# The low parts of the streamed weights beside a recurrence: made by VectorE and not by GpSimd

## The chip, the cores and the metric

The kernel runs on one core of one Trainium2 chip. The metric is the device time of one execution in microseconds, from all inputs in HBM to the whole output in HBM. The engines are named as in the profile: PE is TensorE (PEld its weight loads), DVE is VectorE, ACT is ScalarE, POOL is GpSimd, SP is SyncE, which issues the DMAs. Each engine takes its own queue of instructions in order and waits on semaphores for the others.

## The reference

Two layers on 512 tokens of width 2048, all in float32. The first projects the normed input to 8336 columns (`ab_w_in`) and feeds two branches, 16 heads of attention with a forget gate and 16 heads of a recurrence; both are gated and go through `ab_w_out`. The second is a gated MLP with spatial mixing (`c_w_in`, `c_w_out`). Each layer ends with a norm, a residual and a gated projection. What matters here is the recurrence, for each head a 64x64 state `S` that every token changes:

```python
def step(S, inp):
    r_t, w_t, k_t, v_t, kk_t, a_t = inp
    sa = jnp.einsum('bhij,bhj->bhi', S, kk_t)
    S = S * w_t[:, :, None, :] - sa[..., None] * (kk_t * a_t)[:, :, None, :] + v_t[..., None] * k_t[:, :, None, :]
    y = jnp.einsum('bhij,bhj->bhi', S, r_t)
    return S, y
```

and the projection `proj = xn @ ab_w_in[j]`, whose columns are independent of each other, so that some can be computed while the recurrence runs.

## The kernel before

**Dense products.** Every float32 product with a weight is made of three products of a rounded type: weight and input are split into a high part and a low part, and PE adds high x high, high x low and low x high (L165, L166, L167 in `dense_fm`). The inputs `xh` and `xl` are split once and stay. The weights are streamed: `stream` loads 128x1024 float32 values per DMA (`raw`, two buffers), ACT rounds 128x512 of them to the high part (`whi`, L154), and the engine `self.weng` subtracts it from `raw` to give the low part (`wlo`, L155). `whi` and `wlo` have four buffers each. One such piece serves four k-steps, that is twelve matmuls of `dense_fm`. A column block of 128 takes four pieces.

**Which engine makes the low part.** `self.weng` is an attribute that is set in a few places. In `enter` it is GpSimd for the first two column blocks, but for their first piece; at the end of `enter` (L1243) it becomes VectorE, and so it is for the column blocks that `rwkv_all` makes ahead of its loop (`start(0)`, `start(1)`, one `ahead()`). Right ahead of the loop over the recurrence, L682 sets it to GpSimd. L1269, after `rwkv_all`, sets it back to VectorE for all the rest.

**The recurrence.** The tokens of a pair of heads are taken in eight chunks of 64. For each chunk `rwkv_chain` has three products in a row, each of which needs the one before through a copy out of PSUM: L536 (tile `ch` from the state `SV`), copied to `Bs` by DVE (L539, partitions 0 to 63) and ACT (L540, partitions 64 to 127); L543 with `Bs`, copied to `UV` in the same way (L545 and L546); L551 with `UV`, from which DVE makes the next state `SV` in two halves (L555, two instructions), which the L536 of the next chunk needs. L560 and L561 make the chunk's outputs. Beside the chain the next pair is prepared: `rwkv_prep` (among others L360, L361, L364 and on GpSimd L366, a 128x512 product `a`), `rwkv_ops` (L397, L398, L400, L403, which write `BK` and `AR`; L397 needs the `a` of L366), `rwkv_head` (L423 on PE from `BK` and `AR`), `rwkv_inverse` (the small 32x32 matmuls L490, with the copies L499, L507, L508, L516 and on GpSimd the masks L483) and `rwkv_tokens` (on GpSimd L449, L467 and L468).

**What sets the order.** PE never runs the chain alone. `rwkv_all` gives each step a place on a scale of beats, one beat for each k-step of `dense_fm`, and `beat()` runs the steps that are due, so chain steps and dense matmuls alternate on PE; two chain steps are three beats apart. The dense work is that of the pairs to come (`start(pr + 2)`) and of columns whose results are wanted later (`ahead()`, which parks them in HBM). The program is then scheduled by a list scheduler: it keeps a clock of its own costs and puts on each engine's queue what is ready and has the highest priority. High and low parts have the priority `WPRI` (150000), the chain's copies 60 and the copies of the inverse 80, so that a low part that is ready goes ahead of the chain. After this the queues are fixed.

Of the kernel before, what the change touches and what calls it, by code (L numbers as in the profile page):

```python
# [70 lines left out]
class Net:  # L71
# [522 lines left out]
    def rwkv_all(self, dense, k0, wp, ps):  # L594

        nc, tc = self.nc, self.tc
        sts = {}

        def start(pr):
            sts[pr] = st = {}  # L600
            st["r"] = self.t(wp, [P, T], "r")
            st["k"] = self.t(wp, [P, T], "k")
            st["v"] = self.t(wp, [P, T], "v")
            for c0, m, dst in ((C_RK, 8, st["k"]), (C_R, 0, st["r"]), (C_RV, 16, st["v"])):
                acc = k0 if (pr, m) == (0, 8) else dense(c0 + pr * P)
                with tc.high_priority(HP):
                    self.shifted(acc, m + pr, dst, wp)

        def ahead():

            c0 = AHEAD[len(self.ahead)]
            acc = dense(c0)
            y = self.t(self.wsp, [P, T], "wlo")
            nc.scalar.copy(y, acc)
            self.ahead[c0] = self.gd[len(self.ahead)]
            nc.sync.dma_start(self.ahead[c0], y)

        prep = lambda pr: self.rwkv_prep(pr, sts[pr], wp, ps)
        ops = lambda pr, h: self.rwkv_ops(sts[pr], h, wp)
        head = lambda pr, h: self.rwkv_head(sts[pr], h, wp, ps)  # L620
        tokens = lambda pr, h: self.rwkv_tokens(sts[pr], h, wp, ps)
        inverse = lambda pr: self.rwkv_inverse(sts[pr], wp, ps)
        chain = lambda pr, h: self.rwkv_chain(sts[pr], h, wp, ps)
        fin = lambda pr: self.rwkv_fin(pr, sts[pr], wp, ps)

        start(0)
        with tc.high_priority(HP):
            for gen in (prep(0), ops(0, 0), ops(0, 1)):
                list(gen)
            for h in range(NG):  # L630
                list(head(0, h))
            list(inverse(0))
            list(tokens(0, 0))
        start(1)
        for _ in range(EARLY[0]):
            ahead()

        todo = []

        def put(pr, n, step):  # L640
            todo.append((1 + 2 * WIN * pr + n, step))

        def run(pr, make, *args_places):
            *args, places = args_places
            gen = []

            def step():
                if not gen:
                    gen.append(make(*args))
                next(gen[0], None)  # L650

            for n in places:
                put(pr, n, step)
            put(pr, places[-1], lambda: [0 for _ in gen[0]])

        def begin(pr):
            S0 = sts[pr]["hf", 0]["SV"][:, 0]
            for q in range(2):
                nc.gpsimd.memset(S0[q * 64 : q * 64 + 64, q, :], 0.0)
            sts[pr]["Yt"] = self.t(wp, [P, T], "Yt")  # L660

        for pr in range(8):
            put(pr, CHAIN[0][0], lambda pr=pr: begin(pr))
            run(pr, tokens, pr, 1, TOKENS[1])
            for h in range(NG):
                run(pr, chain, pr, h, CHAIN[h])
            if pr > 0:
                run(pr, fin, pr - 1, FIN)
            if pr < 7:
                if pr == 0:  # L670
                    run(pr, prep, 1, PREP1)
                    run(pr, ops, 1, 0, OPS1[0])
                run(pr, ops, pr + 1, 1, OPS[1] if pr else OPS1[1])
                for h in range(NG):
                    run(pr, head, pr + 1, h, (HEAD if pr else HEAD1)[h])
                run(pr, inverse, pr + 1, STAGE)
                run(pr, tokens, pr + 1, 0, TOKENS[0])
            if pr < 6:
                run(pr, prep, pr + 2, PREP)
                run(pr, ops, pr + 2, 0, OPS[0])  # L680
        self.weave(sorted(todo, key=lambda x: x[0]))
        self.weng = nc.gpsimd  # L682
        for pr, n in enumerate(BESIDE):
            if pr < 6:
                start(pr + 2)
            for _ in range(n):
                ahead()
        self.weave([])
        with tc.high_priority(HP):
            list(fin(7))  # L690
        for _ in range(EARLY[1]):
            ahead()
# [630 lines left out]
```

## Time and profile before

| what | us |
|---|---|
| median of three runs (2384.97 to 2393.15) | 2385.49 |
| the profiled execution | 2386.83 |
| its span, first to last instruction | 2385.1 |
| PE, PEld busy | 2325.8, 1904.0 |
| DVE, ACT, POOL busy | 1172.5, 1046.1, 504.3 |
| mean granted clock of PE | 0.993 |

A row of the order of time gives start, duration, engine, line, operation and tiles; in brackets stands how long the engine stood idle before it and which instruction ended that. A row of waits reads: engine, tile and line of the waiting instruction, those of the one it waited for, then the sum in us, how often, and the longest. A group of instructions gives its count, the busy sum and the mean in ns, and then the engine's idle time ahead of it. A row of stretches gives start and end, length, busy time of PE, PEld, DVE, ACT and POOL with counts, the granted clock of PE, the share of the DMA engines and GB/s. The recurrence lies between 120 and 780 us of the span.

### The profile page before, as it was taken

The page shows a single profiled execution, that of the slowest core. Times are in us where ns is not written, and L with a number is a line of the kernel's source. Part 1 is how long each engine was busy: PE and PEld are TensorE (multiplying, and loading weights), DVE is VectorE, ACT ScalarE, POOL GpSimd, SP SyncE. Part 2 cuts the span into 40 slices and gives each one's busy share as a digit, 9 for nine tenths or more (in the row PEclk, how much of TensorE's full clock was granted, in tenths as well). Part 3 has the DMA queues.
Part 4 walks back from the last instruction along what each step waited for, and adds up shares of the span by engine and source line. Part 5 has one row for each costly group of instructions (what it writes and reads, how often), then busy time and mean ns, then how long its engine had stood idle before and what let it go on. Part 6 is the DMA issues. An engine that isn't in the chain of part 4 may idle for free.

```text
span 2385.1 us, 39010 instructions
## 1 busy us (share of the span) xinstructions
PE 2325.8 (98%) x15356; PEld 1904.0 (80%) x15356; DVE 1172.5 (49%) x2336; ACT 1046.1 (44%) x2135; POOL 504.3 (21%) x488
## 2 busy tenths in 40 slices
PE   6999999999999999999999999999999999999999
PEld 5777877877888777787887888888888888887888
DVE  8644455544511577765227453326544443226433
ACT  5434545554543466665335443323333332335322
POOL 4123443444444000000013110002442000112000
PEclk9999999999999999999999999999999999999999
DMA  6222222223234533326333323233443333232332
GB/s 206 69 77 62 74 79 67 75 59 85 68 89 117 147 93 89 90 83 211 99 102 102 97 89 106 89 97 105 111 111 98 97 97 98 94 104 83 118 114 90
DMA packets 300310, 235.03 MB, mean 99 GB/s; under 512 B 11453, under 2 KB 251214, under 8 KB 299102
## 3 DMA queue, kind: packets, MB, share of 16 engines
q1 hardware_dynamic: 300126, 232.54, 33.3%
q8 instruction: 121, 1.98, 0.3%
q14 instruction: 63, 0.52, 0.1%
HBM read 216.47 MB, written 16.02 MB: 97 GB/s over the span
## 4 chain that ended last, share of the span: by engine, by line
PE 87%; DVE 5%; ACT 3%; issue 1%; DMA 1%; POOL 1%; DVEq 0%; SPq 0%; ACTq 0%; POOLq 0%
PE mm L165 15%; PE mm L167 15%; PE mm L166 15%; PE mm L912 6%; PE mm L914 6%; PE mm L913 6%; PE mm L198 5%; PE mm L200 5%; PE mm L199 5%; PE tm L490 2%; PE tm L828 1%; ACT whi L154 1%; PE mm L1147 1%; PE ch L536 1%; PE tm L423 1%
## 5 line engine op out<-in xcount | busy, mean ns | idle before, releaser
L154 ACT CAST whi<-raw 128x512 fp32r<-128x512 f32 x724 | 447.6, 620 | 883.9 <-PE mm L166 383.3
L155 DVE TENSOR_TENSOR wlo<-raw,whi 128x512 fp32r<-128x512 f32 x566 | 410.2, 727 | 701.3 <-ACT whi L154 686.7
L165 PE MATMUL mm<-xh,whi 128*128 128x512 f32 x1136 | 475.6, 419 | 1.8 <-DVE k L321 1.8
L167 PE MATMUL mm<-xh,wlo 128*128 128x512 f32 x1136 | 452.0, 398 | 0.0
L166 PE MATMUL mm<-xl,whi 128*128 128x512 f32 x1136 | 447.6, 394 | 0.8 <-issue 0.8
L155 POOL TENSOR_TENSOR wlo<-raw,whi 128x512 fp32r<-128x512 f32 x158 | 214.0, 1359 | 260.9 <-ACT whi L154 119.5
L167 PEld LDWEIGHTS mm<-xh,wlo 128*128 128x128 f32 x1136 | 214.7, 189 | 47.8 <-issue 0.2
L165 PEld LDWEIGHTS mm<-xh,whi 128*128 128x128 f32 x1136 | 215.7, 190 | 38.1 <-DVE k L321 1.9
L166 PEld LDWEIGHTS mm<-xl,whi 128*128 128x128 f32 x1136 | 216.0, 190 | 34.1
L165 PE MATMUL mm<-yh,whi 128*128 128x512 f32 x576 | 225.9, 392 | 0.0
L167 PE MATMUL mm<-yh,wlo 128*128 128x512 f32 x576 | 224.3, 389 | 0.0
L166 PE MATMUL mm<-yl,whi 128*128 128x512 f32 x576 | 224.2, 389 | 0.0
L1069 POOL TENSOR_TENSOR accq<-accq,sq 128x512 f32<-128x512 f32 x42 | 56.5, 1346 | 607.1 <-ACT sq L1067 541.8
L914 PE MATMUL mm<-xh,wlo 128*128 128x512 f32 x384 | 149.5, 389 | 0.0
L912 PE MATMUL mm<-xh,whi 128*128 128x512 f32 x384 | 149.4, 389 | 0.0
L913 PE MATMUL mm<-xl,whi 128*128 128x512 f32 x384 | 149.4, 389 | 0.0
L167 PEld LDWEIGHTS mm<-yh,wlo 128*128 128x128 f32 x576 | 108.1, 188 | 22.9
L166 PEld LDWEIGHTS mm<-yl,whi 128*128 128x128 f32 x576 | 108.2, 188 | 22.0
L165 PEld LDWEIGHTS mm<-yh,whi 128*128 128x128 f32 x576 | 108.1, 188 | 22.0
L198 PE MATMUL mm<-whi,xh 128*128 128x512 f32 (+1 forms) x320 | 111.2, 347 | 0.0
L200 PE MATMUL mm<-whi,xl 128*128 128x512 f32 (+1 forms) x320 | 110.9, 347 | 0.0
L199 PE MATMUL mm<-wlo,xh 128*128 128x512 f32 (+1 forms) x320 | 110.9, 347 | 0.0
(362 smaller groups left out, 3868.4 us busy)
## 6 DMA issues: line engine op xcount, KB each, us to landing
raw<-in_ab_w_in_dram SPq DMA_DIRECT2D x130, 512.0 KB, 3.9
raw<-in_c_w_in_dram SPq DMA_DIRECT2D x96, 512.0 KB, 3.8
raw<-in_ple_w_gate_dram SPq DMA_DIRECT2D x64, 512.0 KB, 3.9
raw<-in_ab_w_out_dram SPq DMA_DIRECT2D x32, 512.0 KB, 3.9
raw<-in_c_w_out_dram SPq DMA_DIRECT2D x32, 512.0 KB, 3.9
gd<-wlo SPq DMA_DIRECT2D x21, 256.0 KB, 2.3
vT<-gd SPq DMA_DIRECT2D x21, 256.0 KB, 3.4
xt<-in_x_dram SPq DMA_DIRECT2D x4, 1024.0 KB, 8.4
```

Of the source, the lines that this page charges most:

```text
L154: nc.scalar.copy(hi[:, : m * n], src)
L155: self.weng.tensor_tensor(lo[:, : m * n], src, f(hi[:, : m * n]), ALU.subtract)
L165: nc.tensor.matmul(acc, hi, xhi[k], start=(k == 0), stop=False)
L166: nc.tensor.matmul(acc, hi, xlo[k], start=False, stop=False)
L167: nc.tensor.matmul(acc, lo, xhi[k], start=False, stop=(k == nk - 1))
L198: nc.tensor.matmul(accs[m][:, :n], xh, hi, start=(k == 0), stop=False)
L199: nc.tensor.matmul(accs[m][:, :n], xh, lo, start=False, stop=False)
L200: nc.tensor.matmul(accs[m][:, :n], xl, hi, start=False, stop=(k == nk - 1))
L912: nc.tensor.matmul(accs[j], hi[:, js], xhi[k], start=(k == 0), stop=False)
L913: nc.tensor.matmul(accs[j], hi[:, js], xlo[k], start=False, stop=False)
L914: nc.tensor.matmul(accs[j], lo[:, js], xhi[k], start=False, stop=(k == nk - 1))
L1069: eng.tensor_tensor(accq, accq, sq, ALU.add)
```

## The change

One line goes, so that VectorE stays the engine of the low parts through the recurrence:

```diff
         self.weave(sorted(todo, key=lambda x: x[0]))
-        self.weng = nc.gpsimd
         for pr, n in enumerate(BESIDE):
             if pr < 6:
                 start(pr + 2)
```

Inside the loop and in what follows it in `rwkv_all` 38 column blocks are made, each of four pieces: 152 low parts change their engine. The scheduler orders the queues anew with its costs for the other engine. GpSimd's queue keeps its other instructions in their order (but for one L590), DVE's queue has 152 more, and those of PE and ACT differ at some places. What the order is at two of them:

**Place A**, at the end of a pair's first half, when the next pair is prepared; the same order comes back in three pairs (near 222, 380 and 534 us of the trace). DVE's queue before, where `SV_1586` is the state, `T_2451` the operand of the small matmuls:

```order
L360 TENSOR_SCALAR gn_2395<-a_2254,col_136_517,omka_616 128x512
L400 SCALAR_TENSOR_TENSOR AR_144_536<-kk_2317,Pd_2485 64x4x64
L361 TENSOR_TENSOR k_1551<-k_1551,gn_2395 128x512
L397 TENSOR_TENSOR BK_484_2522<-a_2254,sg_2467 64x4x64
L364 SCALAR_TENSOR_TENSOR rkb_2412<-r_1550,col_136_517,k_1551 128x512
L507 STREAM_TRANSPOSE T_2451<-tm_467_2418 128x256
L398 TENSOR_TENSOR BK_484_2522<-k_1551,sg_2467 64x4x64
L555 SCALAR_TENSOR_TENSOR SV_1586<-SV_1586,PC_831,ch_2458 64x64 x2
L397 TENSOR_TENSOR BK_484_2522<-a_2254,sg_2467 64x4x64
```

and of the changed kernel:

```order
L361 TENSOR_TENSOR k_1551<-k_1551,gn_2395 128x512
L397 TENSOR_TENSOR BK_484_2522<-a_2254,sg_2467 64x4x64
L364 SCALAR_TENSOR_TENSOR rkb_2412<-r_1550,col_136_517,k_1551 128x512
L507 STREAM_TRANSPOSE T_2451<-tm_467_2418 128x256
L398 TENSOR_TENSOR BK_484_2522<-k_1551,sg_2467 64x4x64
L555 SCALAR_TENSOR_TENSOR SV_1586<-SV_1586,PC_831,ch_2458 64x64
L155 TENSOR_TENSOR wlo_2476<-raw_2473,whi_2475 128x512
L155 TENSOR_TENSOR wlo_2529<-raw_2473,whi_2528 128x512
L155 TENSOR_TENSOR wlo_2576<-raw_2573,whi_2575 128x512
L555 SCALAR_TENSOR_TENSOR SV_1586<-SV_1586,PC_831,ch_2458 64x64
L397 TENSOR_TENSOR BK_484_2522<-a_2254,sg_2467 64x4x64
```

Three low parts stand between the two halves of the state. On PE, before:

```order
L551 MATMUL ch_2458<-UV_1585,BKt_1583 128x128
L560 MATMUL ch_2462<-AR_145_537,SV_1586 128x128
L561 MATMUL ch_2462<-GR_879,UV_1585 128x128
L165 MATMUL mm_2472<-xh_85_301,whi_2475 128x512
L166 MATMUL mm_2472<-xl_86_302,whi_2475 128x512
L536 MATMUL ch_2493<-SV_1586,AR_145_537 128x128
L167 MATMUL mm_2472<-xh_85_301,wlo_2476 128x512
```

and changed:

```order
L561 MATMUL ch_2462<-GR_879,UV_1585 128x128
L165 MATMUL mm_2472<-xh_85_301,whi_2475 128x512
L166 MATMUL mm_2472<-xl_86_302,whi_2475 128x512
L490 MATMUL tm_482_2498<-T_2451,A_357_1734 32x32 x15
L167 MATMUL mm_2472<-xh_85_301,wlo_2476 128x512
L165 MATMUL mm_2472<-xh_85_301,whi_2475 128x512
L166 MATMUL mm_2472<-xl_88_307,whi_2475 128x512
L167 MATMUL mm_2472<-xh_85_301,wlo_2476 128x512
L165 MATMUL mm_2472<-xh_85_301,whi_2475 128x512
L166 MATMUL mm_2472<-xl_90_318,whi_2475 128x512
L167 MATMUL mm_2472<-xh_85_301,wlo_2476 128x512
L536 MATMUL ch_2493<-SV_1586,AR_145_537 128x128
```

L536, which needs both halves of the state, has moved behind small matmuls and seven dense ones, the first of which reads `wlo_2476`.

**Place B**, once, early in the recurrence (near 159 us): DVE's queue of the changed kernel from L360 on, where `BK_350` and `AR_146` are what L423 reads. Before, neither low part nor L321 stood ahead of the first L400, which came right behind L360.

```order
L360 TENSOR_SCALAR gn_1659<-a_1607,col_136_517,omka_616 128x512
L155 TENSOR_TENSOR wlo_1844<-raw_1841,whi_1843 128x512
L539 COPY Bs_1713<-ch_1711 64x64
L361 TENSOR_TENSOR k_1263<-k_1263,gn_1659 128x512
L397 TENSOR_TENSOR BK_350_1696<-a_1607,sg_1674 64x4x64
L364 SCALAR_TENSOR_TENSOR rkb_1662<-r_1262,col_136_517,k_1263 128x512
L398 TENSOR_TENSOR BK_350_1696<-k_1263,sg_1674 64x4x64
L545 COPY UV_1251<-ch_1729 64x64
L155 TENSOR_TENSOR wlo_1877<-raw_1841,whi_1876 128x512
L321 SCALAR_TENSOR_TENSOR k_1551<-mm_1553,col_42_136,k_1551 128x511
L400 SCALAR_TENSOR_TENSOR AR_146_538<-kk_1629,Pd_1688 64x4x64
```

On PE the L423 that reads them has moved from behind L543 (chunk's second product) to behind L551:

```order
L551 MATMUL ch_1780<-UV_1251,BKt_1249 128x128
L423 MATMUL tm_361_1738<-AR_146_538,BK_350_1696 128x128 x4
L560 MATMUL ch_1784<-AR_144_536,SV_1252 128x128
L561 MATMUL ch_1784<-GR_855,UV_1251 128x128
L165 MATMUL mm_1759<-xh_85_301,whi_1762 128x512
L423 MATMUL g_1739<-AR_146_538,BK_350_1696 128x128 x4
```

## The prediction

> **What bounds the kernel now.** I read the page first, then the busy time by stretch, then what TensorE (PE) waited for, and last the order of time at its longest waits.
>
> ```profile
> PE 2325.8 (98%) x15356; PEld 1904.0 (80%) x15356; DVE 1172.5 (49%) x2336; ACT 1046.1 (44%) x2135; POOL 504.3 (21%) x488
> ```
>
> PE is busy for 2325.8 of 2385.1 us, so a change on two other engines can only move the 59 us in which PE stands, or the clock at which it runs. The change touches the recurrence, which lies between 120 and 780 us:
>
> ```profile
> 120.00:780.00 660.00, 642.20 (x6994) 518.85 (x6993) 299.36 (x723) 317.67 (x770) 278.21 (x253) 0.98 0.29 79
> ...
> 160.00:170.00 10.00, 7.10 (x31) 5.37 (x30) 9.28 (x18) 2.23 (x6) 5.65 (x4) 0.84 0.29 82
> 170.00:180.00 10.00, 10.00 (x46) 8.03 (x46) 7.79 (x23) 2.33 (x7) 1.29 (x1) 0.82 0.02 6
> 220.00:230.00 10.00, 6.94 (x107) 5.23 (x95) 8.66 (x15) 3.60 (x10) 7.37 (x5) 0.74 0.31 84
> 230.00:240.00 10.00, 10.00 (x81) 8.11 (x78) 2.76 (x8) 4.00 (x10) 0.39 (x1) 0.75 0.18 50
> 530.00:540.00 10.00, 6.86 (x93) 5.08 (x91) 8.64 (x16) 4.27 (x13) 7.38 (x5) 0.94 0.23 62
> 540.00:550.00 10.00, 10.00 (x107) 7.84 (x108) 4.99 (x12) 4.82 (x14) 1.74 (x2) 0.89 0.28 73
> ```
>
> The columns are the length and then the busy time of PE, weight loads, DVE, ACT and POOL, then the granted clock. PE stands 660 - 642.2 = 17.8 us in this stretch. Clock is lost as well, three times right behind a gap: 10 x (0.16 + 0.18) = 3.4 us, 10 x (0.26 + 0.25) = 5.1 us, 10 x (0.06 + 0.11) = 1.7 us, together 10.2 us. So 28 us (1.2%) is all that the change can win. What the 17.8 us waited for, in that stretch:
>
> ```profile
> PE ch L536 <- DVE SV L555: 10.8, 6, 3.1
> PE tm L423 <- DVE BK L398: 2.2, 1, 2.2
> PE ch L543 <- ACT Bs L540: 1.9, 5, 0.7
> PE pp L280 <- ACT a L338: 1.3, 1, 1.3
> PE ch L551 <- ACT UV L546: 1.2, 3, 0.4
> ```
>
> No wait is for a low part: POOL makes them in time. PE waits for the chain's own copies on DVE. The largest looks like this (start, duration, engine; place A):
>
> ```profile
> 219.45 1.93 POOL L366 TENSOR_TENSOR a<-kk,a 128x512 f32<-128x512 f32 x1 [11.17 <-DVE gn L360]
> ...
> 221.25 0.38 PE L551 MATMUL ch<-UV,BKt 128*128 128x128 f32 x2
> ...
> 221.35 4.75 POOL L155 TENSOR_TENSOR wlo<-raw,whi 128x512 fp32r<-128x512 f32 x3
> 221.42 1.49 DVE L397 TENSOR_TENSOR BK<-a,sg 64x256 f32<-64x256 f32 x1 [1.18 <-POOL a L366]
> ...
> 222.15 0.40 PE L166 MATMUL mm<-xl,whi 128*128 128x512 f32 x1
> 222.83 0.73 DVE L364 SCALAR_TENSOR_TENSOR rkb<-r,col,k 128x512 f32<-128x512 f32 x1
> 223.49 0.43 DVE L507 STREAM_TRANSPOSE T<-tm 128x256 f32<-128x256 f32 x1
> 223.86 1.11 DVE L398 TENSOR_TENSOR BK<-k,sg 64x256 f32<-64x256 f32 x1
> ...
> 224.90 0.57 DVE L555 SCALAR_TENSOR_TENSOR SV<-SV,PC,ch 64x64 f32<-64x64 f32 x2
> ...
> 225.61 0.77 PE L536 MATMUL ch<-SV,AR 128*128 128x128 f32 x2 [3.06 <-DVE SV L555]
> ```
>
> It comes back at 383 and 537 us:
>
> ```profile
> 383.61 0.46 PE L536 MATMUL ch<-SV,AR 128*128 128x128 f32 x2 [3.13 <-DVE SV L555]
> ...
> 537.67 0.46 PE L536 MATMUL ch<-SV,AR 128*128 128x128 f32 x2 [3.14 <-DVE SV L555]
> ```
>
> That is 9.33 us in three waits; the other three behind L555 share 1.5 us. At A two DVE instructions are stretched while POOL runs three low parts in a row, L397 to 1.49 us and L398 to 1.11. Over the stretch:
>
> ```profile
> L155 POOL TENSOR_TENSOR wlo<-raw,whi 128x512 fp32r<-128x512 f32 x152 | 203.8, 1345 | 242.4 <-ACT whi L154 100.9 <-PE mm L167 82.9 <-PE mm L166 16.8
> ...
> L397 DVE TENSOR_TENSOR BK<-a,sg 64x256 f32<-64x256 f32 x28 | 21.3, 760 | 7.3 <-POOL a L366 7.1
> ...
> L155 DVE TENSOR_TENSOR wlo<-raw,whi 128x512 fp32r<-128x512 f32 x6 | 4.2, 692 | 11.4 <-ACT whi L154 11.4
> ```
>
> **The change, part by part.** It takes 152 instructions (203.8 us) off POOL and puts 152 x 0.692 = 105 us on DVE, whose load in the stretch goes from 299 to some 404 of 660 us (61%), less what the stretching gives back. Neither sum is on the path; what counts is who is late at PE.
>
> *Place A, three times.* In the order of the changed kernel DVE has L397, L364, L507, L398, one half of L555, three low parts, the other half of L555; PE's L536 stands seven dense matmuls and 15 small ones later, and the dense L167 ahead of it needs the first of these low parts. L397 still waits for L366 on POOL, so it starts at 221.42. Unstretched I take 0.42 for L397 and L398 (L507, of as many elements, takes 0.43): 221.84; L364 +0.73 = 222.57; L507 223.00; L398 223.42; half of L555 (0.28) 223.70; first low part 224.39. PE is through L166 at 222.15 + 0.25 = 222.40, stands 0.65 until L507, works 0.35 on the small ones, and stands about 1.0 for the low part. Two more low parts and the second half of L555 end at 224.39 + 1.38 + 0.28 = 226.05, and PE reaches L536 at 224.43 + 7 x 0.23 = 226.04. So 1.7 us stand there and not 3.1: a gain of 1.4 each, 4.2 in all. The bounds: stretched as now, L397 and L398 cost 1.07 + 0.69 more and nothing is won; with every low part behind L555, 3.1 each.
>
> *Place B, once.*
>
> ```profile
> 159.20 0.55 DVE L360 TENSOR_SCALAR gn<-a,col,omka 128x512 f32<-128x512 f32 x1
> ...
> 159.66 1.50 DVE L400 SCALAR_TENSOR_TENSOR AR<-kk,Pd 64x256 f32<-64x256 f32 x1
> ...
> 161.94 1.51 DVE L364 SCALAR_TENSOR_TENSOR rkb<-r,col,k 128x512 f32<-128x512 f32 x1
> ...
> 162.31 0.43 PE L543 MATMUL ch<-Bs,Tfin 128*128 128x64 f32 x2 [0.69 <-ACT Bs L540]
> ...
> 165.24 1.16 PE L423 MATMUL tm<-AR,BK 64*128 64x128 f32 x8 [2.21 <-DVE BK L398]
> ```
>
> PE stands 0.69 + 2.21 = 2.9 us here. Now two low parts (1.4 us) and L321 come ahead of L400, the stretching (1.50 and not 0.4, 1.51 and not 0.73) goes, and the first L423 stands behind L551, nine dense matmuls after L543. From the end of L360 at 159.75 DVE has two low parts (1.38), L539 and L545 (0.21 each), L361, L364 and L321 (0.7 each, as L364 at A), L397, L398 and L400 (0.42 each): 5.2 us, and some 0.4 waiting for L366 on POOL (1.93 from 159.8), so L400 ends near 165.4. PE asks for it at 162.31 - 0.69 + 0.33 + 9 x 0.23 = 164.0 and stands 1.4. The second group of L423 needs L397, L555, L398 and L400 more (1.8 us, 167.2) and is asked for 1.2 us after the first, near 166.6: 0.6 more. That is 2.0 us where 2.9 were, 0.9 won. Bounds: 0 and 2.9.
>
> *The small waits.* The three that share 1.5 us lose the low parts that stretch DVE, and none is put ahead of them there: 1.5 won. Against that, in the order a low part stands right behind a chain copy, and PE wants it soon, at three places a period apart (some 0.2 each) and at three near the end (0.7, 0.7 and 0.1, by the same counting of rows): 2.1 lost.
>
> *Everywhere else.* Of the chain's 240 DVE instructions 100 get one or more low parts between them and the one before. Behind a low part that waits for its high part the whole DVE queue waits, so each can be 0.7 to 1.4 us late. What covers it is the distance on PE:
>
> ```profile
> 300.13 0.40 PE L166 MATMUL mm<-xl,whi 128*128 128x512 f32 x1
> ...
> 300.36 0.40 PE L167 MATMUL mm<-xh,wlo 128*128 128x512 f32 x1
> ...
> 300.60 0.33 PE L543 MATMUL ch<-Bs,Tfin 128*128 128x64 f32 x2
> ...
> 301.25 0.21 DVE L545 COPY UV<-ch 64x64 f32<-64x64 f32 x1
> ...
> 301.49 0.21 ACT L546 COPY UV<-ch 64x64 f32<-64x64 f32 x1 [0.37 <-DVE UV L545]
> ...
> 303.79 0.38 PE L551 MATMUL ch<-UV,BKt 128*128 128x128 f32 x2
> ```
>
> A dense matmul takes 0.23 us; nine or more (2.1 us) lie between a chain product and the one that uses its copy. Here the copy is there at 301.70 and wanted at 303.79: 2.1 us of cover, more than one low part. I take 0; the bounds are 0 and 100 x 0.69 = 69.
>
> *Clock.* All three losses follow gaps of 2.2 to 3.1 us; 383 us has as long a gap and no loss. With gaps of 1.0 to 1.7 they should come less often; no row shows how much, so I take half of 10.2, 5 us, between 0 and 10.2.
>
> [...]
>
> Sum: -4.2 - 0.9 - 1.5 + 2.1 = -4.5 standing, -5 clock, -9.5 in all: the profiled span of 2385.1 becomes 2375.6. That execution took 2386.83, with 1.7 outside the span; the median of the three runs is 1.3 lower, 2385.49, which gives **2376 us**.
>
> [...]
>
> **The rivals.** *The clock comes back whole.* If no gap is long enough any more, -10.2 replaces -5: 2371 us. For it: the losses stand only behind gaps over 2 us. Against it: place B keeps two gaps close together.
>
> *Nothing is won at A and B.* L366 on POOL (1.93 us) and the pile behind it stay; if a low part's high part is late, L536 waits its 3 us: only the small waits move, by +0.6, to 2386 us. For it: L397 waits for POOL in any case. Against it: these three low parts have had their high parts for long (POOL ran them back to back).
>
> *The chain queues behind low parts (slower).* Engines take their queues in order, and elsewhere DVE stands for its high part a lot:
>
> ```profile
> DVE wlo L155 <- ACT whi L154: 686.7, 375, 8.6
> ```
>
> That is 1.8 us a time over the run. It decides from the point where wait plus 0.69 passes the 2.1 us of cover: if a third of the 100 are 0.7 late at PE, 23 us are lost, 2376 + 23 = 2399 us, more if the clock drops too. For it: this row, and that ACT makes its half of every chain copy from the same kind of queue. Against it: the row tells mostly of a DVE that has nothing else to do; ACT's own high parts stand ahead of the chain's copies already, and PE's waits for L540 and L546 are 1.9 + 1.2 us in the whole stretch.
>
> **How the numbers follow.** Forecast (a small win) 0.50, clock whole 0.20, nothing won 0.18, queueing 0.12. Beyond 0.5%, 12 us, a measurement tells from no change: below 2373.6 or above 2397.4. Faster has the clock's 0.20 and a quarter of the forecast's half, 0.32; slower 0.12; same 0.56. The range goes from 2365 (clock whole and 6 us more of the standing) to 2392 (nothing won, and ten of the 100 places 0.7 late).
>
> **What would show it.** Right: at A, PE waits for L507 and then for a low part, 1.7 us together; L397 and L398 near 0.42; DVE near 400 us between 120 and 780, POOL near 74; PE's standing there near 13.5 us. Wrong: waits of PE for L539, L545 or L555 at many places, DVE held for high parts ahead of them, or L536 still 3 us late.

## The result, and the profile after

| | before | changed |
|---|---|---|
| median of six runs each on one chip, us | 2386.50 (2384.97 to 2393.15) | 2373.36 (2369.15 to 2378.73) |
| ratio, 95% interval | | 0.9932 (0.9916 to 0.9947) |
| the profiled execution, us | 2386.83 | 2378.73 |
| its span, us | 2385.1 | 2377.0 |

The changed kernel is 0.68% faster, 13.1 us; 2376 was forecast. On another chip it came to 0.9936 (0.9917 to 0.9955), with a median of 2373.39. The profiled execution is the slowest of the six, and its clock says why (below).

The busy times of the page:

```profile
PE 2326.1 (98%) x15356; PEld 1904.7 (80%) x15356; DVE 1236.8 (52%) x2488; ACT 1046.4 (44%) x2135; POOL 301.3 (13%) x336
```

The recurrence's stretch, and the 120 us ahead of it, which the change doesn't touch (length, then busy time of PE, weight loads, DVE, ACT and POOL, then the granted clock):

```profile
120.00:780.00 660.00, 651.65 (x7071) 524.78 (x7070) 370.04 (x887) 326.75 (x792) 77.26 (x104) 1.00 0.30 83
0.00:120.00 120.00, 96.18 (x927) 70.69 (x928) 85.67 (x191) 53.65 (x101) 34.01 (x46) 0.90 0.42 132
```

PE stands 8.35 us in the recurrence where it stood 17.8, and its clock is whole there. The low parts now cost DVE 0.70 us each, and the stretched instruction of place A is short again:

```profile
L155 DVE TENSOR_TENSOR wlo<-raw,whi 128x512 fp32r<-128x512 f32 x162 | 110.8, 701 | 76.6 <-ACT whi L154 53.5 <-DMA gd<-wlo 9.3 <-PE mm L167 7.8
L397 DVE TENSOR_TENSOR BK<-a,sg 64x256 f32<-64x256 f32 x28 | 11.9, 424 | 7.3 <-POOL a L366 7.1
```

L397 went from 760 to 424 ns. DVE gained 71 us and not 105: its instructions other than low parts add up to 283 us in this stretch and not to 312 (L397 9.4 us less, L398 4.5, L582 4.2). What PE waits for there:

```profile
PE ch L543 <- ACT Bs L540: 2.5, 4, 0.8
PE mm L167 <- DVE wlo L155: 2.4, 4, 1.1
PE tm L490 <- DVE T L507: 1.3, 3, 0.4
PE pp L280 <- ACT a L338: 1.0, 1, 1.0
PE tm L423 <- DVE AR L400: 0.9, 1, 0.9
```

No wait behind L555 is left. Place A in order of time (here at 222.8 us):

```profile
222.83 1.93 POOL L366 TENSOR_TENSOR a<-kk,a 128x512 f32<-128x512 f32 x1 [11.32 <-DVE gn L360]
...
224.80 0.42 DVE L397 TENSOR_TENSOR BK<-a,sg 64x256 f32<-64x256 f32 x1 [1.18 <-POOL a L366]
...
225.14 0.74 DVE L364 SCALAR_TENSOR_TENSOR rkb<-r,col,k 128x512 f32<-128x512 f32 x1
...
225.53 0.40 PE L166 MATMUL mm<-xl,whi 128*128 128x512 f32 x1
225.81 0.43 DVE L507 STREAM_TRANSPOSE T<-tm 128x256 f32<-128x256 f32 x1
226.17 0.38 DVE L398 TENSOR_TENSOR BK<-k,sg 64x256 f32<-64x256 f32 x1
...
226.30 0.69 PE L490 MATMUL tm<-T,A 32*32 32x32 f32 x30 [0.37 <-DVE T L507]
226.48 0.26 DVE L555 SCALAR_TENSOR_TENSOR SV<-SV,PC,ch 64x64 f32<-64x64 f32 x1
...
226.66 1.88 DVE L155 TENSOR_TENSOR wlo<-raw,whi 128x512 fp32r<-128x512 f32 x3
...
227.40 0.50 PE L167 MATMUL mm<-xh,wlo 128*128 128x512 f32 x1 [0.41 <-DVE wlo L155]
...
229.12 0.38 PE L536 MATMUL ch<-SV,AR 128*128 128x128 f32 x2
```

The place has the shape that the order gave: PE waits for L507, then for the first low part, and L536 waits for nothing. But the two waits are 0.37 + 0.41 us, not 1.7.

**Where the time came from.** All waits of PE in the recurrence, added by place from the order of time of both kernels:

| us that PE stands, 120 to 780 us | before | changed | difference | forecast |
|---|---|---|---|---|
| place A, three times | 9.33 | 2.49 | -6.8 | -4.2 |
| place B | 2.90 | 0.86 | -2.0 | -0.9 |
| L536 behind L555, three others | 1.46 | 0 | -1.5 | -1.5 |
| L551 behind ACT's L546 (three of 0.41) | 1.22 | 0 | -1.2 | 0 |
| L543 behind ACT's L540, elsewhere than B | 1.16 | 2.50 | +1.3 | 0 |
| a low part, elsewhere than A | 0 | 1.12 | +1.1 | +2.1 |
| the rest | 1.72 | 1.29 | -0.4 | 0 |
| sum | 17.8 | 8.3 | -9.5 | -4.5 |

The trace also dates each stretch in which PE was granted half its clock (0.50). In one of them, at 232 us of the kernel before, dense matmuls start 0.43 us apart and not 0.23, so such a stretch costs up to half its length. In the recurrence there were 6.8 + 10.2 + 3.4 us of them before and none now. The profiled execution of the changed kernel lost 8.5 us ahead of the recurrence instead, at 81 us (10.2 us long) and 112 us (6.8 us long), where the queues of both kernels are the same. The second profile of the changed kernel lost nothing at either place, so the change doesn't bring it about; experiment 6 takes it up. This is why its own span fell by 8.1 us only.

For the medians the clock has to be taken over all runs. With span times granted clock as the time without the loss, 49 runs of the kernel before on three occasions have a mean of 2368.5 us and 18.8 lost to the clock; the 12 of the changed kernel 2361.0 and 11.3. So the gain is about 7.5 us of work and waits and 7.5 us of clock, 15 us between these means. (Over its whole span PE stands 8.4 and 9.1 us less in the two profiles of the changed kernel, not 9.5: 0.9 to 1.7 us come back ahead of the recurrence, mostly at 105 to 110 us in waits for which the profile shows no releaser, and 0.6 to 1.3 go behind it. What is left between this and 7.5 stays open.)

### The profile page after: what moved, and what is told of

Its sections match the earlier page's. It is cut to its first block, busy times and chain, and to the rows that moved or that the text cites. A ratio compares the mean times of both kernels' runs of the same rounds, so it can differ in the third digit from the quotient of the medians.

```text
span 2377.0 us, 38890 instructions
## 1 busy us (share of the span) xinstructions
PE 2326.1 (98%) x15356; PEld 1904.7 (80%) x15356; DVE 1236.8 (52%) x2488; ACT 1046.4 (44%) x2135; POOL 301.3 (13%) x336
## 4 chain that ended last, share of the span: by engine, by line
PE 87%; DVE 5%; issue 3%; ACT 2%; DMA 0%; POOL 0%; DVEq 0%; SPq 0%; ACTq 0%; POOLq 0%
PE mm L165 15%; PE mm L167 15%; PE mm L166 15%; PE mm L911 6%; PE mm L913 6%; PE mm L912 6%; PE mm L198 5%; PE mm L200 5%; PE mm L199 5%; PE tm L490 2%; PE tm L827 1%; DVE wlo L155 1%; DVE yh L758 1%; PE mm L1146 1%; PE tm L423 1%
## 5 line engine op out<-in xcount | busy, mean ns | idle before, releaser
L155 DVE TENSOR_TENSOR wlo<-raw,whi 128x512 fp32r<-128x512 f32 x718 | 514.1, 721 | 764.1 <-ACT whi L154 726.0
L154 ACT CAST whi<-raw 128x512 fp32r<-128x512 f32 x724 | 446.9, 620 | 889.1 <-PE mm L166 387.6
L167 PE MATMUL mm<-xh,wlo 128*128 128x512 f32 x1136 | 451.8, 398 | 2.4 <-DVE wlo L155 2.4
L167 PEld LDWEIGHTS mm<-xh,wlo 128*128 128x128 f32 x1136 | 214.3, 189 | 50.6 <-DVE wlo L155 3.1
L167 PE MATMUL mm<-yh,wlo 128*128 128x512 f32 x576 | 224.3, 389 | 0.0
L167 PEld LDWEIGHTS mm<-yh,wlo 128*128 128x128 f32 x576 | 108.1, 188 | 22.9
L198 PE MATMUL mm<-whi,yh 128*128 128x512 f32 x256 | 99.7, 389 | 0.0
```

The lines of the kernel that those rows point to most:

```text
L154: nc.scalar.copy(hi[:, : m * n], src)
L155: self.weng.tensor_tensor(lo[:, : m * n], src, f(hi[:, : m * n]), ALU.subtract)
L167: nc.tensor.matmul(acc, lo, xhi[k], start=False, stop=(k == nk - 1))
L198: nc.tensor.matmul(accs[m][:, :n], xh, hi, start=(k == 0), stop=False)
```

## The experiments

All medians are of 5 to 12 runs. Three groups of runs shared a kernel before: the first four experiments (median 2389.09 us), the next four (2390.00) and the last two (2388.86). Standing is that of PE between 120 and 780 us.

### 1. Place A alone, and all but place A

Theory: the three pairs' place A, where three low parts in a row ran on GpSimd beside L397 and L398, is most of it. Rival: the other 140 low parts matter as much, one by one. The twelve low parts of those three blocks were given to VectorE alone in the first kernel (against the kernel before), and back to GpSimd alone in the second (against the changed one):

```diff
-            for _ in range(n):
+            for j in range(n):
+                self.weng = nc.vector if n == 2 and j == 1 else nc.gpsimd
                 ahead()
+                self.weng = nc.gpsimd
```

```diff
-            for _ in range(n):
+            for j in range(n):
+                self.weng = nc.gpsimd if n == 2 and j == 1 else nc.vector
                 ahead()
+                self.weng = nc.vector
```

> The kernel before, with only the 12 low parts of three column blocks (the second block that is parked ahead in the first, third and fifth pair) on DVE; they hold the three low parts of place A each time, and PE's order at place A is that of the changed kernel. Theory 'place A': the gain sits there, so PE stands some 7 us less than the 17.8 us of before between 120 and 780 us, the half-clock stretches behind place A go, and the time is 2377 to 2380. Theory 'spread' (each of the 152 gives a little): 12 of 152, under 1 us, 2385 to 2386.

> The changed kernel, with those same 12 low parts back on GpSimd. Theory 'place A': three waits of about 3 us for L555 are back, PE stands some 15 us between 120 and 780 us against 8.4, and the time is 2379 to 2383, nearer to before than to the changed kernel. Theory 'spread': 140 of 152 are still moved, 2373 to 2375.

The stretch in the first kernel, then in the second, with the second's longest wait:

```profile
120.00:780.00 660.00, 648.64 (x7045) 522.12 (x7044) 301.26 (x744) 321.82 (x780) 260.69 (x241) 0.99 0.30 82
```

```profile
120.00:780.00 660.00, 645.35 (x7003) 521.64 (x7003) 366.94 (x866) 318.98 (x774) 94.08 (x113) 0.98 0.29 80
```

```profile
PE ch L536 <- DVE SV L555: 9.4, 3, 3.1
```

| | median, us | ratio (95%) | standing | half clock in the recurrence, us from the start (length) |
|---|---|---|---|---|
| place A alone | 2380.48 | 0.9958 (0.9942 to 0.9975) | 11.4 | 167 (6.8) |
| all but place A | 2384.80 | 0.9982 (0.9972 to 0.9991) | 14.7 | 220 (10.2), 377 (3.4), 531 (10.2) |

Twelve of 152 low parts are worth 6.4 us of standing, the other 140 another 3.1, and the two add up to the whole, 9.4. (The 11.4 us contain 0.8 us behind ACT's L710 at 770 us; the kernel before has that wait at 781 us, outside the stretch.) The expected times were counted from 2385.5 us; the kernel before ran at 2389.09 in this group, and against that the two are 8.6 and 4.3 us faster, where the theory of place A had 5.5 to 8.5 and 2.5 to 6.5. The clock follows: with place A mended, the only half-clock stretch left is at place B; with A as before, one stands behind each of its three waits of 3.1 us. That kernel still gains 0.2%, from place B and the small waits.

### 2. Is it GpSimd's instruction, or the order?

The change also put the instructions in another order, so the gain could be the order's. Here the changed kernel keeps its order on PE and DVE at place A, and GpSimd makes the same 152 subtractions once more into a tile that nothing reads (lines behind L155 move by three):

```diff
                     self.weng.tensor_tensor(lo[:, : m * n], src, f(hi[:, : m * n]), ALU.subtract)
+                    if self.extra:
+                        junk = self.t(self.jp, [P, 512], "wjunk", bufs=1)
+                        nc.gpsimd.tensor_tensor(junk[:, : m * n], src, f(hi[:, : m * n]), ALU.subtract)
```

> The changed kernel, where GpSimd makes the same 152 subtractions once more into a tile that nobody reads; DVE still makes the low parts that PE uses, and PE's order at place A is that of the changed kernel. Theory 'DVE is held up by GpSimd's two-input instructions': L397 goes back from 0.42 to 0.7 us or more in the mean, PE stands 5 us or more longer than the changed kernel's 8.4 us, time 2378 or more. Theory 'order' (the gain is that PE's L536 and L423 stand later in the queue): time as the changed kernel, 2372 to 2376.

Measured: 2409.98 us, ratio 1.0080 (1.0064 to 1.0097), some 35 us over the changed kernel by the ratios of both to the kernel before; standing 28.0 us. Place A of this kernel:

```profile
221.56 1.29 POOL L158 TENSOR_TENSOR wjunk<-raw,whi 128x512 f32<-128x512 f32 x1 [3.57 <-issue]
221.69 1.43 DVE L363 TENSOR_SCALAR gn<-a,col,omka 128x512 f32<-128x512 f32 x1
...
225.16 1.27 POOL L158 TENSOR_TENSOR wjunk<-raw,whi 128x512 f32<-128x512 f32 x1
225.24 1.47 DVE L400 TENSOR_TENSOR BK<-a,sg 64x256 f32<-64x256 f32 x1 [1.18 <-POOL a L369]
...
227.78 0.69 PE L493 MATMUL tm<-T,A 32*32 32x32 f32 x30 [2.33 <-DVE T L510]
```

A DVE instruction of 0.42 us (L400 here, L397 before) that starts 0.08 us behind a GpSimd instruction of 1.27 us ends 0.28 us after it. One with a single tensor input, L363, does the same: its mean over the seven is 1.43 us against 0.53 in the changed kernel, and the low parts themselves go from 701 to 821 ns. At place A, PE stands 2.4 to 2.8 us in this kernel, where it stood 3.1 before and 0.8 in the changed one: one stretched instruction there brings back 1.5 to 2.0 of the 2.3 us, and before two were stretched. So the order is not the gain; with the order of the changed kernel, work on GpSimd that nobody waits for costs more than the change won.

This kernel also keeps buffers of the weights longer and has more in GpSimd's queue, so not all of the 35 us need be the stretching. The next experiment gives another dose.

### 3. Half the dose: a copy in place of the subtraction

```diff
-                        nc.gpsimd.tensor_tensor(junk[:, : m * n], src, f(hi[:, : m * n]), ALU.subtract)
+                        nc.gpsimd.tensor_copy(junk[:, : m * n], f(hi[:, : m * n]))
```

> The changed kernel with a copy of each of the 152 high parts made by GpSimd into a tile that nothing reads, in place of the second subtraction of the run before: one input instead of two, the same queue, the same hold on the high parts' buffer (but not on the raw weights'), and a shorter instruction (about 0.75 us, from 0.41 us for half the elements). If VectorE is held up by any GpSimd instruction that reads SBUF, for as long as that lasts, L397 (L400 there) has a mean of 0.50 to 0.60 us against 0.69 with the subtraction and 0.42 without, the low parts 0.74 to 0.79, and TensorE stands 14 to 22 us between 120 and 780 us. Rival: only two-input instructions of GpSimd hold it up: L397 and the low parts keep 0.42 and 0.70, and the standing is within 2 us of 8.35. [...]

```profile
120.00:780.00 660.00, 648.74 (x7037) 521.94 (x7036) 381.13 (x884) 322.34 (x781) 214.53 (x255) 0.99 0.30 82
```

Measured: 2380.14 us, ratio 0.9963 (0.9948 to 0.9978), 6.8 us over the changed kernel run beside it; standing 11.3 us (0.9 of it behind ACT's L711 at 776 us, at the end of the stretch). The copies took 0.91 us each. The copies and two of the instructions beside them, and then L363 beside the subtractions of experiment 2:

```profile
L158 POOL COPY wjunk<-whi 128x512 f32<-128x512 f32 x152 | 138.0, 908 | 364.9 <-ACT whi L154 364.3
L400 DVE TENSOR_TENSOR BK<-a,sg 64x256 f32<-64x256 f32 x28 | 13.1, 466 | 7.3 <-POOL a L369 7.1
L363 DVE TENSOR_SCALAR gn<-a,col,omka 128x512 f32<-128x512 f32 x7 | 5.1, 727 | 0.0
```

```profile
L363 DVE TENSOR_SCALAR gn<-a,col,omka 128x512 f32<-128x512 f32 x7 | 10.0, 1432 | 0.0
```

| GpSimd beside the low parts | L397 (L400), ns | L360 (L363), ns | low part, ns | standing, us | median, us |
|---|---|---|---|---|---|
| nothing (the changed kernel) | 424 | 533 | 701 | 8.35 | 2373.4 |
| 152 copies of 0.91 us | 466 | 727 | 737 | 11.3 | 2380.1 |
| 152 subtractions of 1.55 us | 691 | 1432 | 821 | 28.0 | 2410.0 |

Here one input on GpSimd was enough to stretch DVE (L360 from 533 to 727 ns, L397 from 424 to 466), so the rival of two-input instructions falls. Queue and buffers alone don't account for it either, since durations grow and not waits only. But the standing came out below the 14 to 22 expected and L400 below its 0.50: the stretching grew faster than GpSimd's busy time (L397 by 42 ns beside 138 us of copies, by 267 ns beside 227 us of subtractions). Which share of the last row is due to longer instructions and which to more of them being hit isn't separated.

### 4. Twice the load on VectorE

If the forecast's cover of 2.1 us holds, even twice the low parts on VectorE cost little; if the queue was near its limit, much. Each low part is made twice:

```diff
+                    if self.extra:
+                        self.weng.tensor_tensor(lo[:, : m * n], src, f(hi[:, : m * n]), ALU.subtract)
                     self.weng.tensor_tensor(lo[:, : m * n], src, f(hi[:, : m * n]), ALU.subtract)
```

> The changed kernel, where DVE makes each of the 152 low parts twice in a row: 105 us more on DVE between 120 and 780 us. Theory 'cover' (2.1 us of dense matmuls hide what stands ahead of a chain copy): PE stands at most 10 us longer, time up to 2385. Theory 'the chain queues behind low parts': 100 chain instructions with 0.69 us more ahead of them, a third to all of it on PE, 23 to 69 us, 2396 to 2442.

Measured: 2388.81 us, ratio 0.9999 (0.9987 to 1.0012). The stretch, and the two largest waits (L167 and L543 are two lines lower here):

```profile
120.00:780.00 660.00, 641.12 (x6990) 516.93 (x6989) 452.58 (x1029) 319.33 (x773) 78.45 (x101) 0.99 0.29 79
```

```profile
PE mm L169 <- DVE wlo L157: 10.9, 10, 2.4
PE ch L545 <- ACT Bs L542: 3.0, 4, 1.0
```

PE stands 18.9 us, 10.5 more, for 82 us more of DVE: the second low parts cost an eighth of their own time. Both the 10.5 us and the 2388.81 are a little above the bounds of the theory of cover (10 us, 2385) and far below those of its rival. What comes late is the low part itself (10.9 us, ten times), and hardly the chain. The chain keeps its cover, but the change's gain is gone: the time is 15 us above the changed kernel's, of which the standing explains 10.5 and no view the rest. With 1.4 us a low part instead of 0.70 the change wins nothing; nothing between the two was run.

### 5. What is left at place A: L366, and the copies' priority

The pile at place A still starts with DVE waiting 1.18 us for L366 on GpSimd. One kernel gives L366 to VectorE too; one gives the chain's copies the higher priority, so that both halves of L555 go ahead of the low parts; one does both. The changed kernel ran once more beside the first two.

```diff
-        nc.gpsimd.tensor_tensor(a, kk, a, ALU.mult)
+        nc.vector.tensor_tensor(a, kk, a, ALU.mult)
```

```diff
-CPRI = 60
+CPRI = 2 * HP
```

> The changed kernel with the other instruction on which place A depends, L366 (a = kk*a, 1.94 us on GpSimd, seven of them in the recurrence), on VectorE as well. If place A is a queue on VectorE that still starts with a wait of 1.18 us for L366, L397 starts right behind a 0.7 us instruction of VectorE, the two waits at A (0.37 + 0.41 in the changed kernel) shrink by half or go, and TensorE stands 6 to 7.5 us between 120 and 780 us instead of 8.35; the time is 1 to 3 us below the changed kernel's, which is less than a measurement tells. Rival: seven more instructions of 0.7 us in the queue that now carries everything make other copies late: standing 8.5 to 11, the time 0 to 5 us above.

> The changed kernel with the chain's copies (L538 to L555) given the higher priority of the two, so that low parts stand behind them where both are ready to be placed; at place A VectorE then has both halves of L555 ahead of the three low parts, and TensorE's L536 stands four dense matmuls earlier. If low parts ahead of the chain cost nothing that shows, since the cover is 2 us, the standing between 120 and 780 us stays at 8.35 within 1 us and the time within 0.3% of the changed kernel's. Rival: the queue order is what the rest of the standing is made of (2.5 us behind the ACT copies L540, 2.4 us behind low parts): the standing falls below 6 us and the time by 3 us or more; or, the other way, L536 comes too early and waits up to 1 us each time at A: standing 10 to 12.

> The changed kernel once more, beside the three others. Expected: 0.9932 of the kernel before, within 0.9915 to 0.9950; TensorE stands 7.5 to 9.5 us between 120 and 780 us; the half-clock stretches fall at other places than in the first profile, except that none follows a gap of 3 us at place A, since none is left.

> L366 on VectorE and the chain's copies ahead of the low parts, both at once. Apart they left TensorE standing 4.9 and 8.3 us between 120 and 780 us; the second turned three of the four waits behind the ACT copies L540 (1.8 us) and the waits for low parts at place A (1.3 us) into waits of up to 1.3 us behind L555, which start with the wait for L366. If the two are independent, the L555 waits go with L366 on VectorE and the standing is about 4.9 - 1.8 = 3.1 us, at most 3.7; the time is 1 to 2 us below the version with L366 alone, too little to tell. Rival: with the early place of L536 the L555 waits stay near 1 us each: standing 5 to 7.

> The version with L366 on VectorE once more, beside the one above. Expected: 2369 to 2372 us, ratio 0.992 within 0.990 to 0.994; standing 4.9 us within 0.5 between 120 and 780 us.

| | median, us | ratio (95%) | standing, us | time without clock loss, us | lost to the clock, us |
|---|---|---|---|---|---|
| changed kernel, both groups (12 runs) | 2373.36 and 2373.39 | 0.9932 and 0.9936 | 8.35 and 8.3 | 2361.0 | 11.3 |
| L366 on VectorE | 2370.23 | 0.9920 (0.9901 to 0.9939) | 4.9 | 2359.5 | 9.0 |
| the same again | 2371.23 | 0.9925 (0.9905 to 0.9944) | 4.9 | 2358.6 | 9.9 |
| chain first | 2373.42 | 0.9938 (0.9917 to 0.9960) | 8.3 | 2359.6 | 13.8 |
| both | 2369.08 | 0.9919 (0.9899 to 0.9939) | 3.6 | 2356.5 | 11.0 |

In the second run of the changed kernel and in the last kernel, PE's standing is taken up to 779 us: a wait behind the recurrence (L734, at 779.5 and 779.3 us) falls into the last microsecond of the stretch there.

With L366 on VectorE the waits at places A and B are gone; the longest that are left, in the first kernel of it and then with both:

```profile
PE ch L543 <- ACT Bs L540: 2.4, 4, 0.7
PE mm L167 <- DVE wlo L155: 1.1, 1, 1.1
PE pp L280 <- ACT a L338: 0.9, 1, 0.9
```

```profile
PE mm L167 <- DVE wlo L155: 1.1, 1, 1.1
PE pp L280 <- ACT a L338: 1.0, 1, 1.0
PE ch L543 <- ACT Bs L540: 0.7, 1, 0.7
```

L366 takes 0.68 us on VectorE and 1.9 on GpSimd. The standing fell by 3.4 us, more than the 0.9 to 2.4 expected; 0.9 of it is the wait at place B, which the expectation left out. The copies' priority alone traded one wait for another (L536 behind L555 1.3 us three times, against three of the four waits for L540 and those for L507 and low parts at A); with L366 moved it is worth 1.3 us of standing, 4.9 to 3.6, where 1.2 to 1.8 were expected: the two are nearly independent, and no wait behind L555 is left. The last version has the lowest median of all, 3 to 4 us below the changed kernel by the ratios. Its interval overlaps that of the changed kernel, so that it beats it is not shown by the times; that PE stands 4.7 us less is shown by the traces.

### 6. The clock

The first profile of the changed kernel lost clock ahead of the recurrence. The same 20 us in the kernel before, in that profile, and in the changed kernel's second profile:

```profile
80.00:100.00 20.00, 19.34 (x348) 14.34 (x351) 15.98 (x43) 4.81 (x11) 2.50 (x4) 1.00 0.21 58
```

```profile
80.00:100.00 20.00, 19.39 (x163) 14.37 (x164) 14.32 (x39) 3.45 (x8) 2.04 (x3) 0.74 0.22 57
```

```profile
80.00:100.00 20.00, 19.38 (x291) 14.32 (x295) 16.73 (x44) 4.07 (x11) 3.37 (x4) 1.00 0.22 58
```

PE is equally busy in all three, and its waits there are the same in the two profiles of the changed kernel (0.36, then 0.49 or 0.50 us), but one of them runs 10.2 us at half clock. So a loss also comes without a long wait, in one run and not in the next. (At 112 us the waits do differ: 1.9 us in one piece in the profile that lost clock, 1.3 and 0.5 us apart from each other in the other.)

Counted over all profiled kernels, by what PE stands at place A (all its waits there together; each kernel has the place three times):

| standing at A, us | in which kernels | half clock from it on |
|---|---|---|
| 2.4 to 3.1 | before, all but place A, second subtraction | 8 of 9 |
| 2.0 to 2.1 | low parts twice | 1 of 3 |
| 0 to 1.3 | place A alone, the changed kernel twice, copy, L366 (twice), chain first, both | 0 of 24 |

The table leaves out the other places. With the second subtraction, five waits of 1.7 and 1.8 us elsewhere in the recurrence were followed by half clock three times. What decides between them can be read from the times at which the half clock sets in: in each of the twelve profiles these lie whole multiples of 3.413 us apart (in the kernel before 42, 17, 92 and 158 of them, in the changed one 17, 9, 280 and 58), as if the clock were set anew at fixed moments. Five windows of this grid in the kernel before, at place A the first and the second time (start and end, length, PE's busy time; the granted clock is the third number from the end):

```profile
221.39:224.80 3.41, 1.16 (x9) 0.72 (x7) 3.38 (x4) 1.34 (x4) 3.41 (x3) 1.00 0.00 0
224.80:228.22 3.42, 2.61 (x7) 2.25 (x8) 3.33 (x8) 2.14 (x8) 2.24 (x2) 0.50 0.71 200
378.40:381.82 3.42, 2.09 (x17) 1.52 (x11) 2.39 (x3) 0.62 (x1) 3.42 (x3) 1.00 0.00 0
381.82:385.23 3.41, 1.62 (x8) 1.43 (x9) 3.33 (x8) 2.18 (x7) 2.28 (x2) 1.00 0.40 107
385.23:388.64 3.41, 3.41 (x47) 2.62 (x45) 3.32 (x7) 1.02 (x3) 1.32 (x1) 1.00 0.64 177
```

The first wait of 3.1 us puts 2.25 us of standing into one window, and the next window has half clock. The second is cut by the grid into 1.33 and 1.80 us and loses nothing. In the recurrence of all twelve profiles, all 13 full-clock windows with 1.87 us of standing or more were followed by half clock, 4 of the 6 with 1.58 to 1.80 us, and none with 1.34 us or less (182 such windows in the kernel before, 192 in the changed one). So two waits of 3.1 us lost clock or not by where they fell on the grid. Ahead of the recurrence less was enough: near 80 us, beside small matmuls, six windows with 0.74 to 0.86 us of standing were followed by half clock (one of them from 77.98 to 81.40 us in the changed kernel's first profile, with 0.85), and others with 0.74 and 0.81 were not. That is not explained here.

## Why the prediction was right in its direction and small in its size

**The bound** held: 28 us in the recurrence, of which 9.4 of 17.8 us of standing and all 10.2 us of clock went.

**Place A: the mechanism was right, the term mis-sized.** The forecast had L507, then a low part, then L536 without a wait, and the trace shows these three in this order. But by its own sum the forecast had 0.60 + 1.04 us of standing (it says 0.65 for the first) and the rows have 0.37 + 0.41. From the start of L397 (224.80) L507 ends 1.44 us later and not 1.58, and PE goes on with the low part at 2.60 and not at 2.97: successive DVE instructions overlap. L364 starts 0.34 us behind the start of an L397 of 0.42, and three low parts take 1.88 us, 0.63 each where one alone takes 0.69. The 0.37 us by which L167 goes on earlier are that much of the 0.86 us. Another 0.15 is how the profile counts a standing PE: from the end of a matmul that it shows as 0.40 us long (I took 0.25). The last 0.34 is the cost of the 30 small matmuls, 0.69 us in the row where I took 0.35. The 3.1 us before were counted in the profile's way, so the two didn't match. Experiment 1 shows the term apart from all others: -6.4 from these twelve low parts.

**Place B** gained 2.0 and not 0.9. From the end of L360 (168.30) to that of the first L400 (173.65) it took 5.4 us, near the 5.6 of the sum, but with one term I had not seen:

```profile
168.47 1.57 POOL L366 TENSOR_TENSOR a<-kk,a 128x512 f32<-128x512 f32 x1 [11.23 <-DVE gn L360]
...
169.07 1.52 DVE L361 TENSOR_TENSOR k<-k,gn 128x512 f32<-128x512 f32 x1
...
173.24 0.41 DVE L400 SCALAR_TENSOR_TENSOR AR<-kk,Pd 64x256 f32<-64x256 f32 x1
...
173.70 1.16 PE L423 MATMUL tm<-AR,BK 64*128 64x128 f32 x8 [0.86 <-DVE AR L400]
```

L361 takes 1.52 us beside L366, the instruction that stayed on GpSimd, where the other six of the recurrence take 0.68; the overlaps made up for it. PE asked for L400 at 172.84, 4.5 us behind L360 and not 4.25, and stood 0.86 and not 1.4; the second group found its operands there.

**Small waits.** The three behind L555 went, 1.5 us as forecast. The three of 0.41 us behind ACT's copies L546 went too (1.2 us), which I had quoted and put in no term: a term left out. It is the same stretching: each time, in the kernel before, a DVE instruction ahead of L545 (L430, at 244, 397 and 553 us) takes 1.2 us beside a low part on GpSimd (0.28 at its shortest), and L545, ACT's L546 and L551 come late behind it.

**Low parts ahead of the chain, and everywhere else nothing.** 2.1 us of new waits for low parts were forecast; 1.1 came, at one place near the end (762 us), and 1.3 us of another kind, part of which the rival of the queue describes:

```profile
315.43 0.69 DVE L155 TENSOR_TENSOR wlo<-raw,whi 128x512 fp32r<-128x512 f32 x1
316.15 0.22 DVE L539 COPY Bs<-ch 64x64 f32<-64x64 f32 x1
...
316.41 0.21 ACT L540 COPY Bs<-ch 64x64 f32<-64x64 f32 x1 [0.95 <-DVE Bs L539]
...
316.67 0.43 PE L543 MATMUL ch<-Bs,Tfin 128*128 128x64 f32 x2 [0.75 <-ACT Bs L540]
```

L539 stands behind a low part in DVE's queue, ACT's half waits for L539, and PE waits 0.75 us. That happens at two of the 100 places (0.75 us each). The other two waits for L540 are of ACT's own queue: L540 stands behind a high part (L154) at 551 us, 0.32 us, and behind ACT's copy L614 at 720 us, 0.68 us. With the copies' priority raised (experiment 5) the first three, 1.8 of these 2.5 us, go. At the other places the cover of 2.1 us was enough, as the forecast had it.

**Clock.** I took half of 10.2 us since no row showed how the loss depends on the gap; the half was a guess. All of it went: in the recurrence the rival "the clock comes back whole" was right, in both profiles, as no window of the grid of experiment 6 holds more than 1.2 us of standing there any more. Over the runs it is 7.5 us and not 10.2; only one run of each kernel is traced, so where the others lose it isn't shown. All stretches of half clock in both kernels but the last, cut off by the end, are 3.41, 6.83 or 10.24 us long and set in on the grid of that step. The gap at 383 us, which lost nothing, is cut by it into 1.33 and 1.80 us; 1.87 us of standing in one window was enough each of 13 times.

**The sum.** -4.5 of standing and -5 of clock were forecast, -9.5 together; over all runs it is -7.5 and -7.5, and -13.1 between the medians. Both were small by some 3 us, with the right sign (in the traced recurrence the standing alone fell by 9.5, twice its forecast): 2376 forecast, 2373.4 measured, within 2365 to 2392 and about half way to the 2371 of the rival on the clock. Most of the chance had gone to "within 0.5%", and the gain, 0.68%, lies just outside. Of the rivals, "nothing is won at A and B" fell, since L536 waits for nothing; "the chain queues behind low parts" was right at two places of 100, at 1.5 us; experiment 4 shows that even with 1.4 us a low part it is the low parts that come late and hardly the chain.

GpSimd's remaining work, 77 us in the recurrence, has no term in the sum, but it cost something: at B L366 stretches L361 by 0.8 us, and PE stands 0.86 us behind that queue. What L366 costs at A is its own length, for which DVE waits 1.2 us. With L366 on VectorE both went, 3.4 us of standing; how much of the 0.86 was the stretching isn't separated.

## What to carry to other kernels

An instruction on GpSimd that nobody waits for can still set the time (152 subtractions cost some 35 us in experiment 2): look on VectorE for instructions of one form with two durations (L397: 0.42 and 1.49 us) and at what GpSimd runs in that moment. To move work from GpSimd to a VectorE that was 45% busy paid here where that work stretched a copy on the path, and twelve of 152 instructions at one place carried most of the gain: find that place before moving all. A wait on PE of 2 to 3 us can cost more than itself: half the clock followed 9 of the 12 waits of 2.0 to 3.1 us at place A, once for 10.2 us at a wait of 3.06, which is 5.1 us of clock.

## What the runs showed of the hardware that I had not expected

- A GpSimd copy with one input stretched VectorE too (L360 from 533 to 727 ns in the mean), and beside subtractions a VectorE instruction with one tensor input (L360) was stretched as badly as one with two: 0.53 to 1.43 us, and L397 (L400 there) 0.42 to 1.47.
- VectorE started an instruction about 0.08 us before the recorded end of the one ahead of it (0.34 us from start to start at 0.42 us long), so sums of durations overstated this queue by a tenth or more (three low parts of 0.69 us take 1.88).
- The granted clock changed on a grid of 3.413 us that runs through the whole execution (in the kernel before, half clock set in from 23.4 to 2382.0 us on it). In the recurrence it halved behind each of 13 windows in which PE stood 1.87 us or more, behind 4 of 6 with 1.58 to 1.80 and none with 1.34 or less, so of two waits of 3.1 us one lost 10.2 us of half clock and one nothing. Ahead of the recurrence it also halved behind 0.74 us.
